# Weights times values of the even attention: a three-term split product against one plain float32 product

## The chip, the cores and the metric

The kernel runs on one core of a Trainium2 chip. The metric is the device time of one execution in microseconds; of several runs the median is taken. One further execution was taken with the hardware profiler, and all lines of a trace below come from that one.

Five engines work side by side, each through its own list of instructions in order: PE (TensorE, matrix products and transposes, with PEld for its weight loads), DVE (VectorE), ACT (ScalarE), POOL (GpSimd) and SP (SyncE, which here only issues transfers). They wait for each other through semaphores.

## The reference, cut to what matters

Two layers on 512 tokens and 256 context tokens, width 1024, float32 throughout. Layer 0 (the "even" layer) mixes a gated MLP with a differential attention of 4 heads; layer 1 is a window attention; each is followed by a feed-forward block. The change touches only the last line of this function:

```python
def diff_attn(q, k, v, lam):
    s = jnp.einsum('bqhd,bkhd->bhqk', q, k).astype(jnp.float32) * ATTN_SCALE
    p = jax.nn.softmax(s, axis=-1).reshape(b, B_HEADS, 2, tq, tk)
    a = p[:, :, 0] - lam * p[:, :, 1]
    return jnp.einsum('bhqk,bkhe->bqhe', a.astype(v.dtype), v)
```

In the even layer it is called for 512 queries against 768 keys (tokens and context), and for the 256 context queries against the 256 context keys.

## The kernel before, in words

**Split products.** A large product is done in three matmuls on `float32r` operands: a value is split into a high part (a cast, on ACT) and a low part (value minus high part, on DVE or POOL), and `mm3` adds high x high, high x low and low x high (L99, L100, L101) into one PSUM accumulator. `split` (L113 to L116) makes the two parts: the cast is L115, the subtraction L116. Statistics and transposes use plain `float32` matmuls already (L149, L175, L554, L634, L649).

**The even attention.** Values are projected for six blocks of 128 keys (accumulators `acc`), and each block of 128x512 is split into `vhi` and `vlo` (L497 to L502). Then `head(t)` runs for four heads. A head calls `attend` for three pairs of query blocks (`qp`): two pairs of token queries with six key blocks, one pair of context queries with two. `softmax_diff` makes the scores of one query block (PE L532, L533), their maximum (DVE L534), the exponential with its sum (ACT L536) and the difference of the two softmaxes (DVE L540 to L543). `attend` transposes the weights of two key blocks at a time into one PSUM bank `pt` of 128x512 (PE L554), splits it into `ath` and `atl` (ACT L115, DVE L116), and multiplies with `mm3` (L563), 128 rows by 256 columns, into the accumulator `po`, which ACT copies out (L566). Per head that is 7 such banks and 14 products, in all 28 and 56. Beside it `stack` splits queries and keys for the next head (ACT L268, L269; DVE L257, L271), and `norm` normalises the head before (PE L149, DVE L128 to L132 and L165 on tiles `sm` and `q`, PE L175, DVE L599).

**Work that fills the gaps.** `gated(i)`, eight blocks, each 48 matmuls into the one PSUM bank `pf` (24 of 512 columns, 24 of 256), is put between the heads; ACT copies the result out (L575). `gelu`, `turn` (PE L634, DVE L638 and L639) and `mix` (DVE L648, PE L649, DVE L650) turn these blocks into the other half of the layer's mix. After them DVE and POOL split the results into `ax` (L116, L677), and the output projection reads those (`pw<-ax`, `pb<-ax`).

**The order.** Nobody writes the order of the instructions by hand: the program is scheduled against a timeline, with priorities (`high_priority` for the heads, and `issue_after` for the gelus and heads 2 and 3), and buffers are rings of PSUM banks (`bank`: 3, `wide`: 2, `fill`: 1) and SBUF tiles. So a change of one step changes the order around it.

Of the kernel before, what the change touches and what calls it, by code (L numbers as in the profile page):

```python
# [6 lines left out]
F32 = mybir.dt.float32  # L7
F32R = mybir.dt.float32r
# [6 lines left out]
P = 128  # L15
# [3 lines left out]
TC = 256  # L19
# [7 lines left out]
class Builder:  # L27
# [284 lines left out]
    def even(self):  # L312
        tc, nc, a = self.tc, self.nc, self.a
# [13 lines left out]
        for k in range(0, KT, 2):  # L327
            t = self.load(Rh, a["xT"][k * P:(k + 2) * P, :].rearrange("(k p) t -> p k t", p=P), [P, 2, TX], f"hx{k}")
# [83 lines left out]
        def ada_some():  # L412
            if loaded:
                j, k, t = loaded.pop(0)
                if k == 0:
                    ps_of[j] = self.fill()
                ada_step(ps_of[j], k, t)
                if k == KT - 1:
                    ada_out(j, 2, ps_of.pop(j), self.bank())
# [19 lines left out]
        for half, heads in enumerate(((0, 1), (2, 3))):  # L439
# [3 lines left out]
            for k in range(KT):  # L443
                t = self.adap.tile([P, 2, 512], F32R, name=self.uid("wq"), tag="wq", bufs=3) if k % 3 == 2 else None
# [8 lines left out]
                if half == 0:  # L453
                    t, sh = hx[k], self.modcol(0, 0, k, 0)
# [29 lines left out]
        Rv = tc.alloc_tile_pool(name="v0", bufs=1, side="right", reuse_waits="tile")  # L484


        vhi, vlo = [], []
        acc = [w[:, h * 512:(h + 1) * 512] for w in (self.wide(), self.wide()) for h in range(2)]
        acc += [self.bank() for _ in range(2)]
        for k in range(KT):  # L490
            W = self.unit(a["v0"][k * P:(k + 1) * P, :], 512)
            for tb in range(6):
                c = slice(tb * P, (tb + 1) * P)
                self.mm3(acc[tb], [t[:, c] for t in AX_[k]], W, k == 0, k == KT - 1)
            ada_ahead(1)
            ada_some()
        for ps in acc:  # L497
            h = Rv.tile([P, 512], F32R, name=f"vhi{len(vhi)}")
            l = Rv.tile([P, 512], F32R, name=f"vlo{len(vhi)}")
            self.split(h, l, ps)  # L500
            vhi.append(h)
            vlo.append(l)  # L502
        while rest or loaded:
            ada_ahead(1)
            ada_some()
# [12 lines left out]
        Ra = tc.alloc_tile_pool(name="att0", bufs=1, side="right", reuse_waits="tile")  # L518
        oraw, raw = [], {}

        def softmax_diff(Q, K, qb, eps):


            koff = 0 if qb < 4 else TX
            qs = slice(qb * P, (qb + 1) * P)
            nm, sums = self.small(2, "sa", 10), self.small(2, "sa", 10)
            es = []
            for c in range(2):
                ps = self.wide()
                for p in range(2):  # L530
                    if qb < 4:
                        nc.tensor.matmul(ps[:, :TX], Q[c][:, qs], K[c][p][:, :TX], start=p == 0, stop=p == 1)  # L532
                    nc.tensor.matmul(ps[:, TX:TA], Q[c][:, qs], K[c][p][:, TX:], start=p == 0, stop=p == 1)  # L533
                nc.vector.tensor_reduce(nm[:, c:c + 1], ps[:, koff:TA], axis=AX, op=ALU.max, negate=True)  # L534
                e = Ra.tile([P, TA], F32, name=self.uid("e"), tag="e", bufs=6)
                self.last_exp = nc.scalar.activation(e[:, koff:], ps[:, koff:TA], AF.Exp, bias=nm[:, c:c + 1],  # L536
                                                     accum_out=sums[:, c:c + 1])
                es.append(e[:, koff:])
            r = self.small(1, "sa", 10)
            nc.vector.reciprocal(r, sums[:, 1:2])  # L540
            nc.vector.scalar_tensor_tensor(r, r, self.nlam, sums[:, 0:1], ALU.mult, ALU.mult)
            nc.vector.scalar_tensor_tensor(es[0], es[1], r, es[0], ALU.mult, ALU.add)
            nc.vector.scalar_tensor_tensor(eps[:, qb:qb + 1], sums[:, 0:1], EPS, sums[:, 0:1], ALU.mult, ALU.mult)  # L543
            return es[0]

        def attend(t, Q, K, qp, o, eps):
            es = [softmax_diff(Q, K, 2 * qp + i, eps) for i in range(2)]
            kbs = list(range(6)) if qp < 2 else [4, 5]
            po = self.bank()[:, :TC]
            for i in range(0, len(kbs), 2):  # L550
                pt = self.bank()
                for j in range(2):
                    for b in range(2):
                        nc.tensor.transpose(pt[:, j * TC + b * P:j * TC + (b + 1) * P],  # L554
                                            es[b][:, (i + j) * P:(i + j + 1) * P], self.ident)
                th = Ra.tile([P, 512], F32R, name=self.uid("ath"), tag="at", bufs=6)
                tl = Ra.tile([P, 512], F32R, name=self.uid("atl"), tag="at", bufs=6)
                self.split(th, tl, pt)
                for j in range(2):
                    kb = kbs[i + j]  # L560
                    c = slice(t * P, (t + 1) * P)
                    m = slice(j * TC, (j + 1) * TC)
                    self.mm3(po, (vhi[kb][:, c], vlo[kb][:, c]), (th[:, m], tl[:, m]),  # L563
                             i + j == 0, i + j == len(kbs) - 1)
            s = slice(qp * TC, (qp + 1) * TC)
            nc.scalar.copy(o[:, s], po)  # L566

# [33 lines left out]
        def head(t):  # L601
            Q, K = QK.pop(t)
            o = f3("o", 4)
            eps = self.small(6, "sx", 2)
            for qp in range(3):
                attend(t, Q, K, qp, o, eps)
                if qp == 0:
                    norm(t - 1, 1)
                elif qp == 1:
                    if t < 3:  # L610
                        QK[t + 1] = stack(t + 1)
                    norm(t - 1, 2)
            norms[t] = o, eps
            norm(t, 0)
            if t == 3:
                norm(t, 1)
                norm(t, 2)
            oraw.append(o)
# [718 lines left out]
```

## Time and profile before

| | |
|---|---|
| time, median of 3 runs | 1698.11 us (1692.37 to 1700.24) |
| the profiled execution's own time | 1697.54 us |
| its span, first to last instruction | 1695.8 us |
| busy: PE, PEld | 1558.7 us, 1379.5 us |
| busy: DVE, ACT, POOL | 1145.4 us, 752.8 us, 806.8 us |
| mean clock granted to TensorE | 0.972 |

How to read the lines that follow: a `windows` row gives a stretch of the span in us, its length, then busy us (and instruction count) of PE, PEld, DVE, ACT and POOL, the granted TensorE clock (1.00 is full), and the share and GB/s of the DMA. A timeline row gives start, duration, engine, line, operation, output tile `<-` input tiles, the shape, and in brackets the idle time ahead of it with what ended it. A recorded matmul overlaps its neighbours, so the pace of a stream is read from starts, or from the chain of waits, where each piece counts only what it adds. A plain float32 matmul appears there as two records.

### The profile page before, as it was taken

Reading aid. Unit: us, or ns where it says so; the run is one execution under the profiler, and the core shown is the slowest. Engines: PE = TensorE matmul, PEld = TensorE weight load, DVE = VectorE, ACT = ScalarE, POOL = GpSimd, SP = SyncE. Lnnn points to the kernel's source line nnn. Section 1 sums busy time; section 2 is a strip of 40 time slices with the busy share of each in tenths; the row PEclk is TensorE's granted clock in tenths of the full one; section 3 lists DMA queues with packets and bytes.
Section 4 is the critical chain, followed back from the end, with each engine's and each line's share of the span. In section 5 each row is a group of like instructions: output and inputs, shape, how many; then the busy total and the mean of one; then the engine's idle time right before and its main releaser. Section 6 shows DMA issues by size and latency. Waiting matters only on the chain.

```text
span 1695.8 us, 24602 instructions
## 1 busy us (share of the span) xinstructions
PE 1558.7 (92%) x9415; PEld 1379.5 (81%) x9415; DVE 1145.4 (68%) x2037; ACT 752.8 (44%) x1521; POOL 806.8 (48%) x586
## 2 busy tenths in 40 slices
PE   6999989798899999999999988999987898999996
PEld 4776878698798889888899977778866788888986
DVE  4613788856967677666765676777769865756566
ACT  3413676433533233333333345676655444444443
POOL 0562211232675566656665336512115665666673
PEclk9999989899899899999999999999998999999998
DMA  8753100241032343344341112101140322222311
GB/s 312 290 184 133 32 1 1 87 159 41 25 125 88 124 136 110 127 136 135 132 132 38 49 63 75 51 7 45 50 146 10 125 90 98 87 100 78 110 38 50
DMA packets 47958, 161.98 MB, mean 96 GB/s; under 512 B 5472, under 2 KB 9952, under 8 KB 40160
## 3 DMA queue, kind: packets, MB, share of 16 engines
q1 hardware_dynamic: 47696, 160.28, 27.6%
q8 instruction: 74, 1.21, 0.3%
q14 instruction: 44, 0.36, 0.1%
q10 hardware_dynamic: 144, 0.13, 0.0%
HBM read 158.29 MB, written 2.10 MB: 95 GB/s over the span
## 4 chain that ended last, share of the span: by engine, by line
PE 65%; DVE 18%; DMA 6%; ACT 4%; issue 3%; POOL 3%; POOLq 0%; SPq 0%; DVEq 0%; ACTq 0%
PE pb L100 9%; PE pb L101 9%; PE pb L99 9%; PE pw L99 8%; PE pw L100 8%; PE pw L101 7%; DMA raw<-ffn_in 6%; POOL w L904 3%; DVE t L925 2%; PE pf L99 2%; PE pf L100 2%; PE pf L101 2%; PE pf L349 2%; DVE sq L925 1%; PE pb L1186 1%
## 5 line engine op out<-in xcount | busy, mean ns | idle before, releaser
L78 POOL TENSOR_TENSOR w<-raw,w 128x512 fp32r<-128x512 f32 (+1 forms) x84 | 128.6, 1540 | 234.3 <-ACT w L75 211.8
L99 PE MATMUL pw<-ax,w 128*128 128x384 f32 (+2 forms) x648 | 211.9, 331 | 18.0 <-DVE q L972 5.7
L904 POOL TENSOR_TENSOR w<-t,w 128x512 fp32r<-128x512 f32 x106 | 156.4, 1476 | 149.1 <-ACT w L901 146.0
L100 PE MATMUL pw<-ax,w 128*128 128x384 f32 (+2 forms) x648 | 210.7, 326 | 2.7 <-DVE ax L456 1.4
L101 PE MATMUL pw<-ax,w 128*128 128x384 f32 (+2 forms) x648 | 208.4, 324 | 3.1 <-DVE w L904 3.1
L757 DVE SCALAR_TENSOR_TENSOR xT<-pb,mod,xT 128x512 f32<-128x512 f32 (+3 forms) x208 | 143.9, 703 | 68.3 <-PE pb L101 67.9
L904 POOL TENSOR_TENSOR w<-raw,w 128x512 fp32r<-128x512 f32 x111 | 155.7, 1414 | 59.2 <-ACT w L901 59.2
L99 PE MATMUL pb<-hh,w 128*128 128x512 f32 x480 | 167.4, 363 | 14.8 <-ACT hh L115 7.9
L100 PE MATMUL pb<-hh,w 128*128 128x512 f32 x480 | 172.3, 361 | 0.7 <-POOL hh L116 0.2
L99 PE MATMUL pw<-T,w 128*128 128x384 f32 (+1 forms) x504 | 158.7, 318 | 12.2 <-DVE hs L968 9.5
L101 PE MATMUL pb<-hh,w 128*128 128x512 f32 x480 | 168.7, 359 | 0.0
L901 ACT CAST w<-t 128x512 fp32r<-128x512 f32 x120 | 74.2, 620 | 208.1 <-DVE t L925 176.8
L100 PE MATMUL pw<-T,w 128*128 128x384 f32 (+1 forms) x504 | 159.1, 316 | 7.0 <-DVE T L116 4.1
L101 PE MATMUL pw<-T,w 128*128 128x384 f32 (+1 forms) x504 | 158.3, 314 | 0.0
L99 PEld LDWEIGHTS pw<-ax,w 128*128 128x128 f32 x648 | 125.0, 194 | 32.8 <-DVE q L972 9.2
L100 PEld LDWEIGHTS pw<-ax,w 128*128 128x128 f32 x648 | 125.3, 193 | 10.5 <-DVE ax L193 3.3
L101 PEld LDWEIGHTS pw<-ax,w 128*128 128x128 f32 x648 | 124.8, 193 | 6.4 <-DVE w L904 3.3
L904 POOL TENSOR_TENSOR w<-rawo,w 128x512 fp32r<-128x512 f32 x74 | 107.2, 1448 | 39.1 <-ACT w L901 39.1
L99 PEld LDWEIGHTS pb<-hh,w 128*128 128x128 f32 x480 | 90.6, 191 | 28.5 <-ACT hh L115 9.0
L99 PEld LDWEIGHTS pw<-T,w 128*128 128x128 f32 x504 | 97.3, 194 | 18.9 <-DVE hs L968 11.9
L99 PE MATMUL pb<-ax,w 128*128 128x256 f32 (+1 forms) x344 | 106.8, 313 | 4.1 <-ACT w L75 2.2
L100 PE MATMUL pb<-ax,w 128*128 128x256 f32 (+1 forms) x344 | 106.3, 309 | 2.1 <-DVE ax L116 2.1
(381 smaller groups left out, 4324.4 us busy)
## 6 DMA issues: line engine op xcount, KB each, us to landing
raw<-ffn_in SPq DMA_DIRECT2D x44, 1024.0 KB, 5.7
ar<-ada SPq DMA_DIRECT2D x24, 1024.0 KB, 7.0
ar<-ada SPq DMA_DIRECT2D x48, 512.0 KB, 3.5
rawo<-ffn_out SPq DMA_DIRECT2D x44, 512.0 KB, 3.8
raw<-odd_out SPq DMA_DIRECT2D x32, 256.0 KB, 2.7
raw<-qk SPq DMA_DIRECT2D x16, 256.0 KB, 7.8
raw<-uv SPq DMA_DIRECT2D x16, 256.0 KB, 2.7
raw<-even_out SPq DMA_DIRECT2D x8, 512.0 KB, 3.5
```

Of the source, the lines that this page charges most:

```text
L78: eng.tensor_tensor(lo, raw, hi.bitcast(F32), ALU.subtract)
L99: mm(out, s[0], m[0], start=start, stop=False, **kw)
L100: mm(out, s[0], m[1], start=False, stop=False, **kw)
L101: mm(out, s[1], m[0], start=False, stop=stop, **kw)
L349: nc.tensor.matmul(ps[32 * q:32 * q + 32, :w], cst[:, k, :], t[:, w * q:w * q + w], start=k == 0, stop=k == KT - 1, skip_group_check=True)
L757: self.nc.vector.scalar_tensor_tensor(h, ps[:, r], self.modcol(l, j, m, who), h, ALU.mult, ALU.add)
L901: nc.scalar.copy(t[:, 0, :], src)
L904: eng.tensor_tensor(t[:, 1, :], src, t[:, 0, :].bitcast(F32), ALU.subtract)
L925: nc.vector.tensor_tensor(t, x, y, how)
L1186: nc.tensor.transpose(pt[:, x * P:(x + 1) * P], es[2 * (x % 2) + x // 2][:, kb * P:(kb + 1) * P], self.ident)
```

## The change

The transposed weights in `pt` are copied once as plain `float32` (tile `at`), not split into `ath` and `atl`: by DVE for the middle one of three banks, by ACT otherwise. Each value block is copied once into `V`, by ACT and DVE in turn, not split into `vhi` and `vlo`. Each of the 56 products is one plain `float32` matmul in place of the three of `mm3`. Because two lines go in one place and four in another, what was L554 before is L552 after, and lines behind the change stand 6 lower (L648 is L642).

```diff
-        vhi, vlo = [], []
+        V = []
...
-        for ps in acc:
-            h = Rv.tile([P, 512], F32R, name=f"vhi{len(vhi)}")
-            l = Rv.tile([P, 512], F32R, name=f"vlo{len(vhi)}")
-            self.split(h, l, ps)
-            vhi.append(h)
-            vlo.append(l)
+        for tb, ps in enumerate(acc):
+            v = Rv.tile([P, 512], F32, name=f"v0_{tb}")
+            (nc.vector.tensor_copy if tb % 2 else nc.scalar.copy)(v, ps)
+            V.append(v)
...
-                th = Ra.tile([P, 512], F32R, name=self.uid("ath"), tag="at", bufs=6)
-                tl = Ra.tile([P, 512], F32R, name=self.uid("atl"), tag="at", bufs=6)
-                self.split(th, tl, pt)
+                w = Ra.tile([P, 512], F32, name=self.uid("at"), tag="at", bufs=6)
+                (nc.vector.tensor_copy if i == 2 else nc.scalar.copy)(w, pt)
                 for j in range(2):
-                    kb = kbs[i + j]
-                    c = slice(t * P, (t + 1) * P)
-                    m = slice(j * TC, (j + 1) * TC)
-                    self.mm3(po, (vhi[kb][:, c], vlo[kb][:, c]), (th[:, m], tl[:, m]),
-                             i + j == 0, i + j == len(kbs) - 1)
+                    nc.tensor.matmul(po, V[kbs[i + j]][:, t * P:(t + 1) * P], w[:, j * TC:(j + 1) * TC], start=i + j == 0,
+                                     stop=i + j == len(kbs) - 1)
```

Two places show how the instructions move. The first is PE in head 0, at the first bank of weights that is multiplied (`pb` here is the accumulator; `ath`, `atl`, `at` the transposed weights; `vhi`, `vlo`, `v_` the values). Before, the rows are:

```order
L100 MATMUL pb_1385<-atl_1392,vhi_1271 128x256
L101 MATMUL pb_1385<-ath_1391,vlo_1272 128x256
L99 MATMUL pb_1385<-ath_1391,vhi_1275 128x256
L100 MATMUL pb_1385<-atl_1392,vhi_1275 128x256
L101 MATMUL pb_1385<-ath_1391,vlo_1276 128x256
L554 MATMUL pb_1416<-ident_97,e_1347 128x128
```

And now the same place reads (the transposes are L552 here):

```order
L557 MATMUL pb_1373<-at_1379,v_0_1271 128x256
L557 MATMUL pb_1373<-at_1379,v_1_1273 128x256
L552 MATMUL pb_1383<-ident_97,e_1335 128x128
L552 MATMUL pb_1383<-ident_97,e_1358 128x128
L552 MATMUL pb_1383<-ident_97,e_1335 128x128
```

One row per product stands where three stood, and no row needs a second version of the weights. The first of the three rows of the first product stood further ahead before, between other work.

The second place is DVE at the end of the attention, where head 3 is normalised (`sm`, and L158 which reads its sums of squares) and the mix begins (L648 on tiles `f`, with `sf`). Before:

```order
L648 TENSOR_SCALAR f_374_2099<-f_374_2099,mv,sf_3117 128x128 x6
L158 SCALAR_TENSOR_TENSOR sm_2738<-pb_2739,sx_2457 128x4
L158 SCALAR_TENSOR_TENSOR sm_2738<-pb_2745,sx_2457 128x2
L116 TENSOR_TENSOR ax_3194<-o_1337,ax_3193 128x768
L128 TENSOR_SCALAR sm_2749<-sm_2738 128x6
L130 TENSOR_TENSOR sm_2750<-sm_2749 128x6
L131 SCALAR_TENSOR_TENSOR sm_2750<-sm_2750,sm_2738 128x6
L132 SCALAR_TENSOR_TENSOR sm_2749<-sm_2750,sm_2749 128x6
L650 TENSOR_TENSOR f_353_1910<-pf_3129,sgub_1297 128x512
```

And now, where L642 is the old L648, L593 the old L599 and L644 the old L650:

```order
L131 SCALAR_TENSOR_TENSOR sf_2938<-sf_2938,sf_2935 128x24
L132 SCALAR_TENSOR_TENSOR sf_2937<-sf_2938,sf_2937 128x24
L642 TENSOR_SCALAR f_339_1814<-f_339_1814,mv,sf_2937 128x128 x6
L642 TENSOR_SCALAR f_346_1877<-f_346_1877,mv,sf_2937 128x128 x6
L642 TENSOR_SCALAR f_353_1940<-f_353_1940,mv,sf_2937 128x128 x6
L642 TENSOR_SCALAR f_360_2003<-f_360_2003,mv,sf_2937 128x128 x3
L593 SCALAR_TENSOR_TENSOR o_2318<-o_2318,subg_1299,pb_2589 128x512
L642 TENSOR_SCALAR f_360_2003<-f_360_2003,mv,sf_2937 128x128
L593 SCALAR_TENSOR_TENSOR o_2318<-o_2318,subg_1299,pb_2592 128x256
L642 TENSOR_SCALAR f_360_2003<-f_360_2003,mv,sf_2937 128x128 x2
L116 TENSOR_TENSOR ax_3014<-o_1325,ax_3013 128x768
L644 TENSOR_TENSOR f_339_1814<-pf_2949,sgub_1285 128x512
```

The whole normalisation of head 3 up to its last rows (L593) now stands ahead of the mix's subtractions or among them, and the row that the mix's second half waits for (L644) comes behind all of it.

## The prediction

> **What bounds the kernel now.** I read the page first, then the table of windows, the waits of PE, and the timeline at the two places where PE stands still.
>
> ```profile
> span 1695.8 us, 24602 instructions
> PE 1558.7 (92%) x9415; PEld 1379.5 (81%) x9415; DVE 1145.4 (68%) x2037; ACT 752.8 (44%) x1521; POOL 806.8 (48%) x586
> ...
> 169.00:316.00 147.00, 133.31 (x824) 116.13 (x823) 115.78 (x293) 95.70 (x195) 19.85 (x12) 0.95 0.04 11
> 316.00:326.00 10.00, 9.98 (x62) 8.77 (x60) 9.58 (x42) 4.11 (x6) 0.75 (x1) 1.00 0.73 262
> 326.00:341.00 15.00, 7.11 (x31) 5.81 (x29) 13.37 (x22) 6.69 (x8) 7.99 (x4) 0.66 0.22 70
> ```
>
> The profiled execution took 1697.54 us, 1.7 more than its span, and lies within 0.6 us of the median of 1698.11, so the sum below is made against 1697.54. PE is busy for 92% of the span. The part that changes lies between 163 and 341 us: first the four heads (169 to 316), then the last gated block (to 326), then the step from the mix to the output projection (to 341). In the heads PE is busy for 133.3 of 147 us, so it sits idle for 13.7; its clock is 0.95 on average, which for a clock of either 1.00 or 0.50 means about 15 us at half speed and 7.4 us lost by it. Some 21 us of the 147 are therefore not PE's work. DVE is busy for 115.8 and ACT for 95.7: neither is full, so a second engine bounds the heads only in places.
>
> ```profile
> PE pw L532 <- ACT e L536: 4.7, 4, 1.7
> PE pb L175 <- DVE q L165: 2.6, 1, 2.6
> PE pw L533 <- ACT e L536: 2.5, 1, 2.5
> PE pf L99 <- ACT f L575: 1.3, 1, 1.3
> PE pb L99 <- ACT ath L115: 1.2, 3, 0.7
> PE pb L100 <- DVE atl L116: 0.6, 2, 0.4
> PEld pw L532 <- DVE vlo L116: 0.4, 1, 0.4
> ```
>
> These are PE's waits from 163 to 326 us (total, times, longest). The split itself is a small part: 0.6 us for `atl`, 0.4 us for `vlo`. The greater waits are for the exponentials of ACT (4.7 + 2.5) and for one chain of the normalisation on DVE (2.6).
>
> ```profile
> 228.00:231.00 3.00, 0.88 (x5) 0.44 (x5) 2.88 (x8) 2.67 (x4) 0.00 (x0) 0.99 0.00 0
> 231.00:234.00 3.00, 2.46 (x8) 2.01 (x9) 2.91 (x12) 2.04 (x7) 0.00 (x0) 0.50 0.00 0
> ...
> 234.46 1.28 ACT L622 ACT_TABLE_LOAD   x1
> 235.76 3.05 ACT L622 ACTIVATE f<-f 128x768 f32<-128x768 f32 x4
> 241.74 1.28 ACT L536 ACT_TABLE_LOAD   x1
> ```
>
> Where PE had 0.88 us of work in 3 us, the clock then fell to 0.50. This is between heads 1 and 2, where ACT loads a table, does four gelus (3.05 us) and loads the table of the exponential again; the change leaves this order of things alone.
>
> **The change part by part. PE.** The price of a plain float32 product of 256 columns stands in the trace beside that of a split one, in the chain of waits at 283 us:
>
> ```profile
> 283.37 0.86 PE pb L175 x2
> 284.23 0.12 PE pb L99
> ...
> 284.46 0.12 PE pb L101
> ...
> 284.93 0.43 PE pb L175 x2
> ```
>
> L99 to L101 are one product of the attention, and two of them fill the time from 284.23 to 284.93: 0.35 us each. The L175 rows are plain float32, 512 and then 256 columns against 128 rows; each matmul is two records, and the one of 256 columns, the shape that the change uses, adds 0.43 us. So a product costs 0.08 us more, and 56 of them **+4.5 us** on PE. The low end would be one record only, 0.22 us, which would make it -7.3 us; the operands are of the same type and size as L175's, so I take 0.43 and keep the low end for a rival. [...]
>
> **DVE and ACT.** Means of one, from the groups by shape (163 to 326 us; the last row is of the whole span):
>
> ```profile
> L116 DVE TENSOR_TENSOR atl<-pb,ath 128x512 fp32r<-128x512 f32 x28 | 19.1, 682 | 3.1 <-ACT ath L115 3.1
> L101 PE MATMUL pb<-ath,vlo 128*128 128x256 f32 x56 | 16.1, 287 | 0.0
> L115 ACT CAST ath<-pb 128x512 fp32r<-128x512 f32 x28 | 16.5, 589 | 7.2 <-PE pb L554 7.1
> L575 ACT COPY f<-pf 128x512 f32<-128x512 f32 x8 | 4.7, 588 | 12.8 <-PE pf L101 12.8
> L1161 DVE TENSOR_REDUCE sa<-pw 128x1 f32<-128x512 f32 x32 | 21.8, 684 | 5.8 <-PE pw L1158 5.3 <-ACT q L769 0.5
> ```
>
> DVE loses 28 subtractions of 0.68 (19.1 us) and gets 8 copies. A copy of 128x512 from PSUM on DVE is not in the trace; ACT's takes 0.588, DVE's maximum over the same bank 0.684, so 0.6 to 0.7, and by the nearer engine 0.68: +5.4. For the values it loses six of 0.68 and gets three. In all DVE is relieved of about **15.7 us**. ACT keeps 20 of 28 casts as copies of the same 0.59 and three of six for the values: **6.5 us** less. None of this is time saved by itself; it is worth what of it lay on the path. The chain of waits holds these pieces of `atl` in the heads, the first and the last of five, 3.1 us together:
>
> ```profile
> 197.09 0.61 DVE atl L116
> ...
> 292.07 0.60 DVE atl L116
> ```
>
> Of the five, one was a bank's middle one at most, where a copy by DVE takes its place; I count **-3.1** for them, **-0.4** for `vlo`, and **-1** for half-speed clock behind those waits. What is late next in the same places is `e` (ACT L536) and the first copy, which stays where L115 was. The other 11 us that DVE no longer does are hidden today beside PE's products and stay so. If they were all on the path, it would be a rival below.
>
> **The end of the heads.** In the new order the sums of head 3 are made after the last product and before the last gated block, so PE waits there for ACT's copy of `o` (256 columns), its square (768) and the release of the one `pf` bank (a copy of 256); by L575's 0.588 for 512 that is an estimate of 0.3 + 0.9 + 0.3. Some small transposes fall into it, and the old order hides the sums in the block. I take **+1** (0 to +2.5).
>
> **The step to the output projection.** Here DVE and POOL block each other today:
>
> ```profile
> 302.70 0.17 DVE L132 SCALAR_TENSOR_TENSOR sm<-sm,sm 128x6 f32<-128x6 f32 x1
> 302.90 1.27 DVE L165 TENSOR_SCALAR q<-ident,sm 128x128 f32<-128x128 f32 x6
> ...
> 239.35 2.81 DVE L165 TENSOR_SCALAR q<-ident,sm 128x128 f32<-128x128 f32 x6
> ...
> 318.69 6.24 DVE L648 TENSOR_SCALAR f<-f,mv,sf 128x128 f32<-128x128 f32 x24
> 325.25 4.14 POOL L116 TENSOR_TENSOR ax<-o,ax 128x768 fp32r<-128x768 f32 x2 [52.93 <-ACT ax L115]
> 325.86 1.80 DVE L128 TENSOR_SCALAR sm<-sm 128x6 int32<-128x6 int32 x1
> 329.35 4.64 POOL L78 TENSOR_TENSOR w<-raw,w 128x1024 fp32r<-128x1024 f32 x2
> 331.75 2.26 DVE L132 SCALAR_TENSOR_TENSOR sm<-sm,sm 128x6 f32<-128x6 f32 x1
> 333.94 0.68 DVE L650 TENSOR_TENSOR f<-pf,sgub 128x512 f32<-128x512 f32 x1
> 334.67 1.22 PE L649 MATMUL pf<-sguT,f 128*128 128x128 f32 x4 [6.91 <-DVE f L650]
> 338.13 0.67 PE L99 MATMUL pw<-ax,w 128*128 128x384 f32 x1
> ```
>
> Four operations of POOL take 8.7 us (325.25 to 334.0), and in that time DVE gets four small ones done, 1.8 to 2.3 us each, where the same takes 0.17 at 302.70. PE idles 6.9 us for it. In the new order the normalisation comes first, but the 24 subtractions (L648, 0.26 each) stand where it stood. Counted from the end of the last gated block in both: POOL starts 0.7 us before it, as today, because its inputs need the same release; DVE, which first does the chain of head 3 (some 24 small ones of 0.17 and L165's 1.27, 5.4 us), has about 15 of 24 subtractions done by then, four more between POOL's operations, and five (1.3 us), L599 and L116 (2.0 us) after them. So the bank is released 11.4 us after the block, not 8.0; on the other hand the projection (`pw<-ax`) then starts at once, where today it begins 4.2 us after that release (333.94 to 338.13). I take **+1** (-7 to +4).
>
> [...]
>
> **The sum.** +4.5 (PE) - 4.5 (waits and clock) + 1 (end of the heads) + 1 (step) = +2, that is 1697.5 + 2 = **1699.5 us**.
>
> A later place moves as well: at 1280 us, in the second feed-forward block, a dozen DVE rows change places.
>
> ```profile
> 1280.00:1320.00 40.00, 27.63 (x156) 25.14 (x156) 38.73 (x59) 21.43 (x49) 26.64 (x22) 0.79 0.08 27
> ```
>
> DVE is full there (38.7 of 40 us), so an exchange of two neighbours of 0.4 to 1.4 us can shift PE by as much; I give it 0, with 3 us to either side.
>
> **The rivals.** *DVE was the bound (faster).* If the 15.7 us of DVE lay on the path and the half-speed clock went with the waits, up to 17 of the 21 lost us would go: 1697.5 + 4.5 + 2 - 17 = 1687. For it: DVE is at 2.88 and 2.91 of 3 us where the clock falls. Against it: PE's greatest waits name ACT's `e`, and ACT's gelus stand in between. It decides for "faster" if more than 14.5 us of waits go. [...] 0.13.
>
> *The product is dearer and nothing pays for it (slower).* PE gets +5, no wait goes since `e` is as late as before and only the path's last step changes its name, the end of the heads gives +2.5, and the subtractions behind POOL give +4: 1697.5 + 11.5 = 1709. It decides from +8.5 us, which needs the step to cost its upper end. For it: the waits on `atl` are only 0.6 us by name. Against it: the five pieces on the chain. 0.18.
>
> *The subtractions are not held up by POOL.* Then the bank is released some 7 us sooner than counted: 1692.5. For it: L648 has never met POOL in this trace; against it L165 and L128, of the same operation. 0.12.
>
> *The plain product is one record here, not two.* Then PE gains 7.3 where I count 4.5 of loss: 1687.7; L175's rows speak against it. 0.02. *The late exchange decides*, by 3 us either way around 1699.5: 0.07.
>
> **How the numbers follow.** The forecast has 0.48. About 0.5% (8.5 us) is what a measurement of this kernel can tell from no change. Faster by more are the first and the fourth rival, 0.15; slower by more the second, 0.18; the rest, 0.67, lies within. The range goes from 1688, which leaves out some half of the first rival, to 1710, just above the second with its late exchange: 0.08 and 0.09 are left out.
>
> **What would show it.** Right: L557 appears 112 times on PE, two records a product, 0.43 us each in the chain; from 169 to the last product the clock again falls between heads 1 and 2; DVE's busy time up to 326 us is some 16 us less; L642 rows of 1.5 to 2.3 us alternate with POOL's. Wrong: a clock of 1.00 in all the heads (the first rival), L642 at 0.3 beside POOL (the third), or PE waits on `at` (L555) of several us, which I count at no more than L115's 1.2 today.

## The result and the profile after

The changed kernel takes **1705.17 us** (median of 20 runs, 1699.28 to 1711.00) where the kernel before takes 1699.32 (20 runs). The ratio is 1.0037, with a 95% interval of 1.0027 to 1.0047: slower by 5.9 us, inside the 0.5% that was called no change. The profiled execution took 1710.46 us, so it stands 5.3 us above its own median; single executions of either kernel differ by 12 to 13 us, and what follows therefore rests on stretches of a trace that repeat, not on the ends of two traces.

The top of the page of the changed kernel:

```profile
span 1708.6 us, 24460 instructions
PE 1561.7 (91%) x9359; PEld 1377.8 (81%) x9359; DVE 1129.6 (66%) x2014; ACT 745.8 (44%) x1510; POOL 805.8 (47%) x586
```

DVE has 15.8 us less work, ACT 7.0 less, PE 3.0 more. The new instructions, from the rows by line and shape (count, then min/median/max in ns, then the first and last start):

```profile
L557 PE MATMUL pb<-at,v x112: 377/379/483, 186.6 to 318.4; 128*128 128x256 f32 x112
L555 ACT COPY at<-pb x20: 565/586/599, 184.0 to 315.0; 128x512 f32<-128x512 f32 x20
L555 DVE COPY at<-pb x8: 659/680/692, 188.9 to 306.2; 128x512 f32<-128x512 f32 x8
```

The 56 products are 112 records, and eight records in a row add 1.73 us to the chain of waits, 0.43 a product. DVE's copy out of PSUM takes 0.68, as taken. Now the stretch of the heads (first scores to last product), first of the kernel before, then of the changed one, and in the last row the stretch from there to the end of the last gated block of the changed kernel:

```profile
168.80:316.00 147.20, 133.51 (x824) 116.33 (x824) 115.98 (x293) 95.84 (x195) 19.85 (x12) 0.95 0.04 11
```

```profile
170.70:318.60 147.90, 132.53 (x764) 112.63 (x763) 104.29 (x262) 90.54 (x185) 17.93 (x12) 0.98 0.05 16
318.60:333.40 14.80, 12.11 (x71) 10.12 (x69) 12.08 (x64) 5.32 (x9) 0.77 (x1) 1.00 0.34 123
```

The heads take 147.9 us where they took 147.2. PE's waits in and just behind them (total, times, longest):

```profile
PE pw L530 <- ACT e L534: 7.0, 4, 4.9
PE pw L531 <- ACT e L534: 3.5, 3, 2.3
PE pb L557 <- DVE at L555: 1.6, 2, 1.4
PE pb L149 <- ACT sq L585: 1.5, 1, 1.5
PE pf L99 <- DVE sm L132: 1.2, 1, 1.2
PE pb L557 <- ACT at L555: 1.0, 3, 0.5
```

The exponentials `e` stay first, with 10.5 us where it was 7.2, and the single copy `at` still makes PE wait 2.6 us. At the end of the heads the kernel before had these rows on PE: the transposes of the last `turn` (L634, on the one bank `pf`), the last product, and the first matmul of the last gated block:

```profile
312.48 0.60 PE L634 MATMUL pf<-ident,f 128*128 128x128 f32 x4
314.68 0.44 PE L634 MATMUL pf<-ident,f 128*128 128x128 f32 x2
315.90 0.28 PE L101 MATMUL pb<-ath,vlo 128*128 128x256 f32 x1
316.20 0.47 PE L99 MATMUL pf<-ax,w 128*128 128x512 f32 x1
```

After the change, from the last product (318.37) on, PE first, then DVE, then POOL (the transposes are L628 here):

```profile
318.58 0.60 PE L628 MATMUL pf<-ident,f 128*128 128x128 f32 x4
320.71 1.60 PE L149 MATMUL pb<-ones,sq 128*128 128x128 f32 x12 [1.53 <-ACT sq L585]
322.15 0.38 PE L628 MATMUL pf<-ident,f 128*128 128x128 f32 x2
323.69 0.47 PE L99 MATMUL pf<-ax,w 128*128 128x512 f32 x1 [1.16 <-DVE sm L132]
329.26 1.46 PE L175 MATMUL pb<-q,ones 128*128 128x512 f32 x4
342.32 1.22 PE L643 MATMUL pf<-sguT,f 128*128 128x128 f32 x4 [7.12 <-DVE f L644]
343.19 0.67 PE L99 MATMUL pw<-ax,w 128*128 128x384 f32 x1
...
333.29 1.27 DVE L642 TENSOR_SCALAR f<-f,mv,sf 128x128 f32<-128x128 f32 x1
334.86 3.77 DVE L642 TENSOR_SCALAR f<-f,mv,sf 128x128 f32<-128x128 f32 x2
338.55 3.11 DVE L116 TENSOR_TENSOR ax<-o,ax 128x768 fp32r<-128x768 f32 x1
341.58 0.68 DVE L644 TENSOR_TENSOR f<-pf,sgub 128x512 f32<-128x512 f32 x1
...
332.63 3.61 POOL L116 TENSOR_TENSOR ax<-o,ax 128x768 fp32r<-128x768 f32 x2 [57.93 <-ACT ax L115]
336.20 4.65 POOL L78 TENSOR_TENSOR w<-raw,w 128x1024 fp32r<-128x1024 f32 x2
```

The sums of head 3 (L149) and its spread (L175) now stand between the last product and the mix, with two waits. So do the transposes (L628), which stood ahead of the last product before; the last gated block, which needs the same bank, starts 5.3 us after the last product where it started 0.3 after it. (The gated block ahead of these transposes leaves the bank later: ACT's copy of it starts at 317.92, before the change at 311.65.) Then POOL runs for 8.2 us, and in that time DVE gets three of the L642 and one L116 done, beside the two rows of L593; the L116 takes 3.11 where 0.95 is usual. PE stands still for 7.1 us, as it did for 6.9 before.

From here on, stretches of the even layer are measured between these starts, in each kernel's own profile (so the heads are 147.6 us here and 147.9 in the window, which runs to the product's end): first scores, last product, mix's first product, mix's first addition (L644, L650 before), first residual of the output projection.

| profile | heads | to mix | to addition | to residual | sum |
|---|---|---|---|---|---|
| before | 147.1 | 10.7 | 7.3 | 40.2 | 205.3 |
| after | 147.6 | 15.7 | 7.5 | 37.8 | 208.7 |

### The profile page after: what moved, and what is told of

Its sections match the earlier page's. It is cut to its first block, busy times and chain, and to the rows that moved or that the text cites. A ratio compares the mean times of both kernels' runs of the same rounds, so it can differ in the third digit from the quotient of the medians.

```text
span 1708.6 us, 24460 instructions
## 1 busy us (share of the span) xinstructions
PE 1561.7 (91%) x9359; PEld 1377.8 (81%) x9359; DVE 1129.6 (66%) x2014; ACT 745.8 (44%) x1510; POOL 805.8 (47%) x586
## 4 chain that ended last, share of the span: by engine, by line
PE 63%; DVE 18%; DMA 6%; ACT 4%; POOL 4%; issue 4%; POOLq 0%; SPq 0%; DVEq 0%; ACTq 0%
PE pb L100 8%; PE pb L99 8%; PE pb L101 8%; PE pw L99 7%; PE pw L100 7%; PE pw L101 7%; DMA raw<-ffn_in 6%; POOL w L898 3%; DVE t L919 3%; PE pf L99 3%; PE pf L100 2%; PE pf L101 2%; PE pf L349 2%; DVE junk L220 1%; PE pb L1180 1%
## 5 line engine op out<-in xcount | busy, mean ns | idle before, releaser
L78 POOL TENSOR_TENSOR w<-raw,w 128x512 fp32r<-128x512 f32 (+1 forms) x84 | 126.2, 1510 | 238.4 <-ACT w L75 232.3
L898 POOL TENSOR_TENSOR w<-t,w 128x512 fp32r<-128x512 f32 x106 | 155.0, 1463 | 150.8 <-ACT w L895 147.6
L99 PEld LDWEIGHTS pw<-ax,w 128*128 128x128 f32 x648 | 125.2, 194 | 35.5 <-DVE q L966 11.4
L99 PE MATMUL pb<-ax,w 128*128 128x256 f32 (+1 forms) x344 | 108.1, 317 | 4.2 <-ACT w L75 2.2
L99 PEld LDWEIGHTS pw<-T,w 128*128 128x128 f32 x504 | 96.6, 193 | 16.0 <-DVE hs L962 9.9
L100 PEld LDWEIGHTS pw<-T,w 128*128 128x128 f32 x504 | 96.8, 192 | 15.5 <-POOL T L116 7.5
```

The source lines that it names most:

```text
L78: eng.tensor_tensor(lo, raw, hi.bitcast(F32), ALU.subtract)
L99: mm(out, s[0], m[0], start=start, stop=False, **kw)
L100: mm(out, s[0], m[1], start=False, stop=False, **kw)
L898: eng.tensor_tensor(t[:, 1, :], src, t[:, 0, :].bitcast(F32), ALU.subtract)
```

## The experiments

All were timed in three sets, each beside the kernel before on the same chip; ratios are to it, with 95% intervals. In these sets the kernel before had medians of 1699.03, 1698.41 and 1699.76 us. The first expectation counts the even layer to a residual row some 2 us behind the table's.

**The changed kernel again**, no edit.

> The changed kernel once more, to see which of its extra time comes again. Theory A (the extra time is made in the even layer): from the first scores to the first residual of the even layer it takes 3.4 us more than before (210.8 against 207.4), and from there to the end no more than 3 us more than before's 1319.6. Theory B (the moved rows of the second feed-forward block, or something else late, carry the extra time): from the first residual to the end it takes 5 to 8 us more again, as in the first profile (1327.1). The ratio of times stays near 1.0037 under both.

Measured: 1707.05 us, ratio 1.0038 (1.0020 to 1.0055). Its profile repeats the even layer: 147.7, 15.7, 7.5, 37.7, in sum 208.6. Outside that layer it was again long, as in the first profile (670 us from the residual to the next layer's scores, 457 from that layer's last transpose to the end, where the kernel before has 665 and 450), but it was a long execution too (1713.85 us). So A's price of the even layer stands and B is not yet out.

**The kernel before again**, no edit.

> The kernel before once more, unchanged, for a second profile of it. Theory A (the stretch from the first scores of the even layer to the first residual is 3.3 us longer after the change, and the rest of the 12.8 us between the two profiles is the spread of single executions): this profile shows the stretch again at 205 to 206 us, while the time outside it differs from the first profile by several us, 1696 to 1704 us in all. Theory B (the change costs time behind the even layer as well): this profile's late stages lie within 1 us of the first one's, 665 us from the first residual to the second layer's first scores and 450 from its last transpose to the end. In the first profile VectorE gave way to GpSimd at 452 us (its sum of squares took 1.50 us, GpSimd's subtraction for T 1.37); in all five profiles of changed kernels GpSimd waited for VectorE there instead (8.53 us for two subtractions). By theory B this profile shows the first of these again; by theory A it may show either. Ratio to before 1.000.

Measured: 1698.05 us, ratio 1.0002 (0.9990 to 1.0014). Even layer 205.9 us (147.3, 10.7, 7.3, 40.6), as A says; so by the second pair of profiles the change costs 2.7 us there, by the first 3.4. The late stages were 665.7 and 448.5, so they do not differ by several us here, as A wanted, and at 453 us the row looks like that of the changed kernel, against B. The same program has shown both forms. VectorE and GpSimd start within some 0.05 us of each other there; in the first profile of before GpSimd got through at once and VectorE's next row was held (1.50 us where 0.68 is usual):

```profile
452.00 0.55 DVE L116 TENSOR_TENSOR ax<-hh,ax 128x384 fp32r<-128x384 f32 x1
452.04 1.37 POOL L116 TENSOR_TENSOR T<-hh,T 128x384 fp32r<-128x384 f32 x1 [2.71 <-ACT T L115]
452.46 1.50 DVE L925 TENSOR_TENSOR sq<-raw 128x512 f32<-128x512 f32 x1
```

In the second, VectorE went on without a gap and GpSimd waited:

```profile
453.28 0.55 DVE L116 TENSOR_TENSOR ax<-hh,ax 128x384 fp32r<-128x384 f32 x1
453.33 8.53 POOL L116 TENSOR_TENSOR T<-hh,T 128x384 fp32r<-128x384 f32 x2 [2.71 <-ACT T L115]
453.75 0.68 DVE L925 TENSOR_TENSOR sq<-raw 128x512 f32<-128x512 f32 x1
```

Between the two profiles of before, the second falls back 1.5 us on VectorE and 2.6 on TensorE from 450 to 466 us by this, and has made up most of it at 583 (0.4 behind). The form with the wait came in most profiles of changed kernels, but one of them (POOL out of the step, below) shows GpSimd through in 1.37 us at 449.07. So either form can come with either order, and no cost of the change is shown at that place.

**One term.** The product of the high parts alone, which leaves the two low-part terms out of the weights times values:

```diff
-            v = Rv.tile([P, 512], F32, name=f"v0_{tb}")
+            v = Rv.tile([P, 512], F32R, name=f"v0_{tb}")
...
-                w = Ra.tile([P, 512], F32, name=self.uid("at"), tag="at", bufs=6)
+                w = Ra.tile([P, 512], F32R, name=self.uid("at"), tag="at", bufs=6)
```

> The changed kernel with the weights and the values cast to the split format and only one matmul per product: high x high alone, the two terms with low parts are left out. Copies, banks and their number stay. PE has 56 x (0.43 - 0.12) = 17.4 us less to do. Theory (PE is on the path for most of the heads): the stretch from the first scores to the last product falls by 9 to 17 us, the time by as much. Rival (the heads are bound by the chain of maximum, exponential and gelu on ACT and DVE, and PE's price is hidden in its waits): it falls by less than 6 us.

Measured: 1698.88 us, ratio 0.9998 (0.9983 to 1.0013). The heads fall to 144.5 us only, by 3.2, which is the rival's side. The whole falls by 6.8 us against the changed kernel of the same set (1.0038), because the stretches behind the heads moved as well (18.4, 3.0 and 37.6, in sum 203.5 against 208.7). The window of the heads:

```profile
170.40:314.90 144.50, 124.65 (x707) 105.83 (x705) 101.55 (x261) 89.88 (x185) 19.05 (x12) 0.91 0.03 10
```

**Each product twice.** The other direction; sums of products are doubled by it.

```diff
+                    for n in range(2):
-                    nc.tensor.matmul(po, V[kbs[i + j]][:, t * P:(t + 1) * P], w[:, j * TC:(j + 1) * TC], start=i + j == 0,
-                                     stop=i + j == len(kbs) - 1)
+                        nc.tensor.matmul(po, V[kbs[i + j]][:, t * P:(t + 1) * P], w[:, j * TC:(j + 1) * TC],
+                                         start=i + j + n == 0, stop=n == 1 and i + j == len(kbs) - 1)
```

> The changed kernel with each of the 56 plain products issued twice in a row, so that what they add up to is doubled: 24.1 us more for TensorE at 0.43 us a product. Theory A (between first scores and last product the pace is set by the chain of maxima, exponentials and copies, and TensorE's time counts little on either side, as the 17.4 us left out brought 3.1): the stretch of 147.7 us grows by 4 to 8 us. Theory B (at 89% busy TensorE is close to the bound: time taken off finds the chain, time put on finds TensorE): it grows by 16 to 22 us, and the whole takes 1722 to 1728. The prediction's term of +4.5 us, counted in full, belongs to B.

Measured: 1718.40 us, ratio 1.0107 (1.0088 to 1.0125). The heads take 161.1 us, 13.5 more than after the change, between A and B:

```profile
170.10:331.20 161.10, 153.98 (x874) 133.90 (x873) 104.06 (x262) 91.20 (x185) 19.52 (x12) 0.99 0.04 12
```

The four windows of the heads together say how PE's time is paid for. Idle is the length less PE's busy time. The clock's loss is one less the granted clock, times the length, give or take 0.7 us for rounding; where the clock is low while PE is idle, up to some 2 us are counted twice. The rest is PE's work at full clock.

| us in the heads | length | work at full clock | idle | lost by the clock |
|---|---|---|---|---|
| one term | 144.5 | 111.6 | 19.9 | 13.0 |
| before | 147.2 | 126.2 | 13.7 | 7.4 |
| after | 147.9 | 129.6 | 15.4 | 3.0 |
| each twice | 161.1 | 152.4 | 7.1 | 1.6 |

Of 18.0 us of work taken off, 4.5 turned into idle time and 10.0 into a lower clock. Of 22.8 us put on, 8.3 were found in idle time; the clock's 1.4 is within the error. Neither side is free and neither is paid in full. How the loss divides between idle time and clock changes from one execution to the next: in four profiles with the heads of before, idle is 12.4 to 15.3 us and the clock's loss 4.4 to 8.9; in five with the changed heads 14.4 to 15.4 and 3.0 to 4.4. Their sum is steady, 19.7 to 21.6 and 18.2 to 18.8. One term also makes the matmuls `float32r` ones; whether the kind of matmul has a part in the clock was not tried apart.

**The subtractions kept.** The changed kernel, with a subtraction on DVE behind each copy whose output nobody reads:

```diff
+                x = Ra.tile([P, 512], F32, name=self.uid("ax_"), tag="sub", bufs=2)
+                nc.vector.tensor_tensor(x, pt, w, ALU.subtract)
```

> The changed kernel with the 28 subtractions of the transposed weights kept on DVE (into a tile that nobody reads); the plain product stays. DVE gets 19 us of work back in the heads. Theory (DVE's relief is mostly hidden): the stretch from the first scores to the last product grows from 147.9 us by 1 to 4 us. Rival (DVE was the bound and its relief paid for the dearer product): it grows by 9 us or more.

Measured: 1705.62 us, ratio 1.0039 (1.0025 to 1.0053); heads 149.2, so 1.5 us more for the 28 subtractions (19.1 us by 0.68 each):

```profile
169.60:318.80 149.20, 134.81 (x767) 113.98 (x766) 119.10 (x294) 91.50 (x186) 19.44 (x12) 0.98 0.04 11
```

DVE's relief was worth 1.5 us of 19, as the theory says. Behind the heads the sums of head 3 stand in the gated block again, as before the change (13.1, 7.6, 39.4), which makes the sum 209.2.

**Head 3's sums at their old place.** Two `norm` calls are moved behind the gated block's first matmuls.

```diff
-            if t == 3:
-                norm(t, 1)
-                norm(t, 2)
...
+        with tc.issue_after(self.last_g.ins):
+            norm(3, 1)
+        norm(3, 2)
```

> The changed kernel with the sums of head 3 (L149) and what follows put behind the first half of the last gated block, where they stood before the change; all computation stays. Theory A1 (the wait of PE between the last product and the last gated block costs its whole length): the stretch from the last product to the end of the gated block falls from 14.8 to about 10.5 us, the step behind it loses the 2 us that it had won, and the time falls by 2 to 3 us against the changed kernel, ratio to before about 1.002. Rival (what is won there is given back in the step to the projection, since DVE and POOL block each other again): 0 +- 1 us.

Measured: 1704.53 us, ratio 1.0032 (1.0017 to 1.0047); 148.2, 14.5, 8.5, 40.0, in sum 211.2. In the even layer the block's side gains 1.2 us, the step loses 3.2 and the heads 0.5, which speaks for the rival. The time is 2.5 us below that of the changed kernel in the same set, but the intervals overlap, so it decides nothing. The place of the sums, then, is not the main thing that lengthened the end of the heads from 10.7 to 15.7. What stays there are the transposes of the `turn` (L627 here), now with waits for DVE's statistics:

```profile
317.87 0.60 PE L627 MATMUL pf<-ident,f 128*128 128x128 f32 x4
320.27 0.41 PE L627 MATMUL pf<-ident,f 128*128 128x128 f32 x2 [1.80 <-DVE mv L632]
321.77 0.47 PE L99 MATMUL pf<-ax,w 128*128 128x512 f32 x1 [1.08 <-DVE mv L632]
```

The last gated block starts 4.1 us after the last product, against 5.3 and, before the change, 0.3. Putting the transposes back ahead of the last product was not tried.

**POOL out of the step**, in both kernels, by the same edit:

```diff
-            self.split(*cat[k], src, nc.gpsimd if k in (5, 6) else nc.vector)
+            self.split(*cat[k], src, nc.vector)
```

> The changed kernel, with the two subtractions for heads' outputs 5 and 6 at the step to the output projection on VectorE instead of GpSimd. Theory (VectorE's small operations at 333 to 338 us, 1.3 to 2.4 us each, are held up by GpSimd's two subtractions and the two for weights behind them): VectorE takes 2 x 0.95 us more, GpSimd's 3.6 us go, its weight subtractions come that much sooner, TensorE's 7.1 us idle at 342 us falls to about 4, and the kernel gains 2 to 3 us on the changed one (1704 where that has 1707). Rival: the weight subtractions on GpSimd hold up the same small operations, only sooner, and the time stays within 1 us.

> The kernel before, with the same two subtractions on VectorE instead of GpSimd. Theory (as for the changed kernel): the small operations of 1.7 to 2.3 us at 326 to 334 us shrink to 0.2 us, up to 4 us come off the step, and the kernel runs at about 1696. [...]

Measured: the changed kernel with it 1697.84 us, ratio 0.9996 (0.9982 to 1.0010); the kernel before with it 1698.43, 1.0001 (0.9988 to 1.0013). In the changed kernel the step's rows are now:

```profile
331.14 0.34 DVE L642 TENSOR_SCALAR f<-f,mv,sf 128x128 f32<-128x128 f32 x1
331.79 0.59 DVE L642 TENSOR_SCALAR f<-f,mv,sf 128x128 f32<-128x128 f32 x2
332.30 2.69 DVE L116 TENSOR_TENSOR ax<-o,ax 128x768 fp32r<-128x768 f32 x3
333.72 17.43 POOL L78 TENSOR_TENSOR w<-raw,w 128x1024 fp32r<-128x1024 f32 x6 [61.19 <-ACT w L75]
334.91 0.68 DVE L644 TENSOR_TENSOR f<-pf,sgub 128x512 f32<-128x512 f32 x1
```

L642 takes 0.3 instead of 1.3 to 2.4, three L116 take 0.9 each instead of one 3.11, and when POOL's weights come, at 333.72, DVE has its 24 subtractions done; PE's 7.1 us wait is gone from the list, and the sum of the stretches is 202.5 (147.6, 15.7, 3.0, 36.2), 6.2 less than after the change. That is more than the 2 to 3 us of the theory. In the kernel before the weights' subtractions hold DVE's small rows all the same:

```profile
328.20 4.66 POOL L78 TENSOR_TENSOR w<-raw,w 128x1024 fp32r<-128x1024 f32 x2 [56.11 <-DVE f L650]
328.30 2.28 DVE L131 SCALAR_TENSOR_TENSOR sm<-sm,sm 128x6 f32<-128x6 f32 x1
330.62 2.27 DVE L132 SCALAR_TENSOR_TENSOR sm<-sm,sm 128x6 f32<-128x6 f32 x1
```

There the sum is 206.2 (147.2, 10.7, 1.2, 47.1) and nothing is gained, against the theory. The weights come at the same point of the step in both, 1.8 to 1.9 us after the mix's first product (331.88 and 326.31). What differs is what DVE still has to do then: in the changed kernel head 3's chain is over, in the kernel before its small rows are yet to come.

**POOL out of two subtractions for `T`** in the first feed-forward block of the changed kernel:

```diff
-        lo_eng = {5: "PPDD", 6: "PDPP", 3: "DDDD", 7: "PDDP", 4: "DDPD"}
+        lo_eng = {5: "PPDD", 6: "PDPP" if l else "PDDD", 3: "DDDD", 7: "PDDP", 4: "DDPD"}
```

> The changed kernel, with two subtractions for T in the first FFN (those that took 8.53 us together on GpSimd at 458 us) on VectorE. Theory (there the changed kernel loses 3 us against before's profile, because a run of VectorE operations without a gap keeps GpSimd from its two subtractions and TensorE waits 3.8 us for them): the wait goes, VectorE takes 1.1 us more, and the kernel gains 1 to 3 us on the changed one. Rival: the loss at 458 us is made good by 583 us anyway, where other waits end later, and the time stays within 1 us.

Measured: 1699.84 us, ratio 1.0012 (1.0001 to 1.0023), even layer unchanged at 209.0. Against the first profile of before it stands 2.8 us nearer at 583 us than at 376, where the changed kernel stands 0.9 further; the rest of its 5 us falls outside that stretch and is not placed. The gain is larger than the theory's 1 to 3 us. It does not show a cost of the change: by the runs of both kernels with and without it (next, and above), the same edit is worth about as much in the kernel before: 1.0001 to 0.9978 beside the other pair, as far as two sets can be compared.

**Both moved**, in the changed kernel and in the kernel before.

> The changed kernel with both pairs of subtractions moved from GpSimd to VectorE: the two at the step to the output projection and the two for T in the first FFN. Theory (the two gains lie in different places and add): the first alone was worth 8 us between the changed kernel and it (1705 to 1707 against 1698), the second 5 to 7; the second's own place, 452 to 583 us, shows 2 to 3 of it, so 1695 and at the best 1693, below both kernels. Rival: what the second was worth lay in the spread of the stages behind, and nothing is added (1698).

> The kernel before with the same two pairs of subtractions on VectorE. Theory (the change itself pays in the even layer once GpSimd is out of the step: first scores to first residual is 202.5 us with it and 206.2 without, so 3.7 us): this one takes 1696 to 1697, and the changed one with both moved is 1.5 to 4 us faster. Rival: the 3.7 us do not reach the end, and both take the same.

Measured: the changed kernel with both 1694.63 us, ratio **0.9965** (0.9952 to 0.9979); the kernel before with both 1696.50, 0.9978 (0.9965 to 0.9991). The even layer takes 202.5 us in the one and 206.5 in the other, so the change itself gains 4.0 there. The medians differ by 1.9 us, as this theory has it, but their intervals overlap, so that a gain of the change reaches the end is not shown. The kernel with both moved is below both kernels of this study.

## Why the prediction was right, and where not

The forecast was +2 us, within 0.5%; +5.9 was measured, within 0.5% and inside the range. By the profiles the sum's own stretch, first scores to first residual, came out at +3.4 (+2.7 by the second pair). That this is near +2 is in part luck, as the terms show:

- **PE, +4.5.** Price and count were right: two records, 0.43 a product. Work at full clock in the heads grew by 3.4 us. No run shows the half microsecond by which the second rival's +5 lies above 4.5: eight L557 records in a row add 1.73 us, the 0.43 a product of the forecast.
- **Waits and clock, -4.5.** The size was near for a wrong reason. The waits were to give 3.5 us and the clock 1. In this pair of profiles idle time grew by 1.7 and the clock's loss fell by 4.4, together -2.7; only this sum is steady from profile to profile. The wait on `atl` went, but a wait of 2.6 us on the single copy `at` came (I had allowed 1.2), and `e` grew to 10.5 from 7.2. With PE's term the heads came out at +0.5 by their starts (+0.7 by the windows) where 0 was forecast. That some of PE's term is paid back is no accident, as the four windows show: idle time and the clock's loss together shrink when PE's work grows.
- **End of the heads, +1.** The step that failed most: 15.7 us against 10.7, so +5.0, with two waits of 1.5 and 1.2 (1.5 in all had been counted). L175 (1.46) moved in, which stood in the output projection before, at 339.56. But with the sums and L175 moved out again, 14.5 remain. What stays are the transposes of the `turn` and their statistics, ahead of the last product before and behind it now, in the one bank that the last gated block needs. I had seen that small transposes fall into this place and gave them no price.
- **The step, +1.** It came out at -2.1 (45.4 against 47.5), inside the ends I gave. The release of the bank comes 8.2 us after the block, not 11.4: DVE had 21 of its 24 subtractions done when POOL started, not 15, since head 3's chain was over by then. Three are held up by POOL, at up to 2.38 us each, where four between its operations and five behind them were forecast. This error and the one before lean on each other: the sums and L175 that came forward to the end of the heads were gone from the step. So their errors, +4.0 and -3.1, nearly cancel, and the sum gains by that without having foreseen it.
- **The clock** did fall again between heads 1 and 2, from 1.00 to 0.50 at 243.67, in a wait of 4.93 us for `e` that ends at 247.41, after ACT's four gelus (3.04 us), four rows of casts and copies and a table load (1.28 us). Each row is a window of 3 us, the granted clock third from its end:

```profile
243.00:246.00 3.00, 0.00 (x0) 0.00 (x0) 2.16 (x2) 2.93 (x5) 1.81 (x1) 0.61 0.00 0
246.00:249.00 3.00, 1.59 (x5) 1.27 (x6) 2.10 (x11) 2.99 (x7) 0.00 (x0) 0.50 0.00 0
```

- **The late exchange, 0 within 3.** No cost of it is shown. The kernel with one term has the changed kernel's late order and takes 666.6 and 450.2 us for the two late stages, as the kernel before does with the other order. The kernel with the subtractions kept has the late order of before, and is as slow as the changed one.

That leaves some 2.5 to 3 of the 5.9 us. Both profiles of the changed kernel reach the first scores 1.6 to 1.9 us later than those of before, ahead of any changed instruction, and run long in the late stages (668.8 and 454.3, then 669.9 and 456.9), but both are long executions of it. The kernel with one term is as late at the first scores (170.4) and not long behind. No changed instruction makes this lateness: it is there whole on PE at 40 us, and the first changed copy starts at 165.39. Six variants with the same instructions up to the first scores on PE, DVE, ACT and POOL reach them at 168.6 to 170.1 us, the kernels with the order of before at 168.4 to 169.0. What makes the late stages of the changed kernel long stays open.

Of the rivals, the first (DVE was the bound) is out: 19 us of DVE's work brought 1.5. The second had the sign and half the size, and was right that PE's idle time in the heads would not fall; it left out the clock, which gave back most of PE's term, and its +4 for the step was -2.1. The third was right in part: PE's idle time there stayed at 7.1 us, but 21 of 24 subtractions did not meet POOL.

That POOL would hold up L642 was an estimate from L128 and L165: in the kernel before L165's six took 2.81 us at 239.35, with POOL's L257 (1.83 us) starting at 239.67, and 1.27 at 302.90 with POOL idle. The rows of the step show the same (L642 at up to 2.38 us beside POOL, 0.34 without it). The rows at 453 us show the other side: with VectorE's rows end to end, GpSimd's first subtraction took 7.59 us in the chain of waits, where it takes 1.37 when it gets in.

## What to carry to other kernels

When an engine is 90% busy and waits the rest, its work has no fixed price: in these heads a microsecond taken off PE brought 0.2 and one put on cost 0.6, so such a term is counted with a share, not in full or not at all. When an edit moves a small chain to another place, price its instructions and not its waits alone, and what else shares its buffer, and look for the idle time that they leave. A change can lose or win by what runs beside it: this one was 0.37% slower, and with two pairs of subtractions taken off POOL it was 0.35% faster than the kernel before, which the same two moves alone made 0.22% faster.

## What the runs showed of the hardware

Less work for PE went with a lower clock: with 18 us taken out of a stretch of 148, the granted clock went from 0.98 to 0.91, and 10 of the 18 us were lost to it. PE did not stand still all the time ahead of such a fall: in the kernel before the clock fell to 0.50 at 230.96 and at 241.20 us, and in the 3.00 us ahead of each PE had been busy for 0.92 and 1.09 us. What sets the clock back was not shown.

Which of VectorE and GpSimd got through first can't be told from the starts that the traces show. At 452 us the same program once let GpSimd through in 1.37 us and once kept it for 8.53 (two subtractions), with starts 0.04 and 0.05 us apart, and a changed kernel let GpSimd through at 0.05. In the changed kernel's profile the held-up subtraction is the third longest piece of the whole chain of waits (start, us, what), and yet, 5.3 us behind the first profile of before at 376 us, this profile is only 6.2 behind at 583:

```profile
457.92 7.59 POOL T L116
...
782.21 7.65 DMA raw<-ffn_in
...
1511.04 7.68 DMA raw<-ffn_in
```
